# Loading x first, and computing some adaLN rows on TensorE, in the opening of a hybrid decoder block

## The chip, the cores and the metric

The kernel runs on one core of a Trainium2 chip. Its time is the device time of one execution in microseconds. Three runs of the kernel before took 1878.87 to 1883.16 us, median 1879.36.

The engines named here: TensorE (PE; its weight loads are PEld) multiplies matrices; VectorE (DVE) and ScalarE (ACT) work elementwise; GpSimd (POOL) does a few small operations; SyncE (SP) issues DMAs. Each runs its own queue in order and waits on the others through semaphores.

## The reference

One decoder block on x (1024 tokens, 1024 features, float32). Only its first lines matter for this change:

```
mod = silu(c) @ w_ada + b_ada                  # 6 x 1024 values for the sequence
sh1, sc1, g1, sh2, sc2, g2 = split(mod, 6)
h = rms_norm(x, pre_norm1_w) * (1 + sc1) + sh1
proj = h @ w_in                                # z, xbc, dt, q, k, v, gates
```

Then follow a Mamba-2 branch and a differential-attention branch on the parts of proj, their merge by sigmoid gates, an output projection, and a gated convolutional feed-forward network, each with a norm around it. In the attention branch a constant, lambda, is the difference of the exponentials of two dot products of 64 elements.

## The kernel before

All large products are float32 split in two: a high part rounded to a type that TensorE takes at full pace (float32r), and a low part, the difference. A product of two such operands is three TensorE products (high x high, low x high, high x low).

The opening (lines 151 to 324) makes h, transposed (features on partitions), in 16 **units**: 8 feature blocks k of 128, times 2 token halves of 512. It also multiplies each unit by the first three weight blocks (two of w_xbc, one of w_gate), so that TensorE has work while h is made. By steps:

- `load_x`, `square_x`, `rstd_x`, `scale_x`: eight tiles of x (128 tokens x 1024), each 512 KB, are loaded; ScalarE sums their squares; VectorE and GpSimd make the reciprocal root; ScalarE or VectorE scales each tile. A half is four tiles.
- `load_mod(j)`: the two 128-column strips of w_ada that give shift and scale of feature block j, 1 MB, by four DMAs of 256 KB in runs of 512 bytes, into eight buffers (four blocks).
- `mod_sum(j, k)`: VectorE multiplies the k-th 128 rows of these strips by silu(c) and adds them up: eight operations on 128 x 256, and one more that joins two partial sums. `mod_cols(j)`: two TensorE products with a column of ones sum over the partitions and leave shift and scale as columns. `mod_end(j)`: three tiny VectorE operations add the bias and apply the norm weight. Block 0 has a form of its own, `mod_first`: shift by TensorE, with the strips as stationary operand, scale by VectorE.
- `make_h(k, half)`: four TensorE transposes; ScalarE applies scale and shift into float32 (line 240) and rounds a copy of that to the high part (line 241); VectorE subtracts for the low part (line 242).
- `products(k, half)`: nine TensorE products (lines 256 to 258), accumulated over the units in PSUM.

The order within the opening is written out by hand for TensorE, VectorE, ScalarE and SP (`tc.manual_schedule`). Loads: half one of x, block 0 of w_ada, the three weight blocks, block 1, half two of x, blocks 2 and 3, then one w_ada block each time a block has been summed. Units: (0,0), (1,0), (0,1), (1,1), then by block. In unit n TensorE transposes unit n and then runs the products of unit n-1, while VectorE does four sums. A scheduler merges this list with the code that follows it, so that some later instructions stand among those of the opening on VectorE, ScalarE and SP: constants for lambda (lines 1256 to 1260, written after the chunk stage, in no list of their own), a copy of `sel` (line 341), the split of the second w_gate block (lines 93 and 94) and some differences of h (line 557). SP waits, for each DMA, for the one eight before it.

After the opening TensorE goes on to the other w_gate blocks (lines 115 to 117), then to the projections by a Strassen-like scheme, the chunk stage of the Mamba branch, attention, and the feed-forward network.

## Time and profile before

| what | value |
|---|---|
| median of 3 runs | 1879.36 us (1878.87 to 1883.16) |
| profiled execution: time | 1882.31 us |
| profiled execution: span | 1880.2 us |
| TensorE busy | 1837.8 us, 98% |
| VectorE busy | 1301.7 us, 69% |
| ScalarE busy | 889.7 us, 47% |
| mean granted TensorE clock | 0.999 |

A row of the timeline gives start and duration in us, the engine, the source line, the operation, what it writes and reads, the shape, the count of merged instructions, and in brackets how long the engine was idle before it and what ended that. A TensorE product's duration holds the way through the array, so that products overlap: their pace is read from one start to the next. Rows of the windows give, for each stretch, its length and the busy time and instruction count of each engine, the granted clock, the busy share of the DMA engines and what they moved. A row of a group gives smallest, median and largest duration.

### The profile page before, as it was taken

How to read it: one execution, taken by the hardware profiler on the slowest of the kernel's cores; microseconds unless marked ns; L12 is line 12 of the kernel's file. 1: busy time of each engine (PE TensorE's matmuls, PEld its weight loads, DVE VectorE, ACT ScalarE, POOL GpSimd, SP SyncE). 2: the span in 40 equal slices, each digit the busy share in tenths (PEclk: the TensorE clock that was granted, in tenths of full speed). 3: DMA queues.
4: the chain of work that ended last, by engine and by line, in shares of the span. 5: the costliest groups of instructions: out<-in, count | busy, mean ns of one | idle time of the engine just before them, and what ended most of it. 6: DMA issues, size and time to landing. Idle time of an engine off the chain costs nothing.

```text
span 1880.2 us, 24563 instructions
## 1 busy us (share of the span) xinstructions
PE 1837.8 (98%) x9032; PEld 1535.6 (82%) x9032; DVE 1301.7 (69%) x1987; ACT 889.7 (47%) x1718; POOL 145.2 (8%) x137
## 2 busy tenths in 40 slices
PE   6999999999999999999999999999999999999998
PEld 4788889987888888888888888888888888887886
DVE  6777877689755247777667465478898888876545
ACT  5644543345443025656556323465554545455532
POOL 0000000145521000000000000000000000000001
PEclk9999999999999999999999999999999999999999
DMA  9356356678837746666543755122232323278844
GB/s 307 129 180 211 101 177 206 208 275 284 292 118 179 232 140 174 172 192 167 146 135 109 244 190 219 45 90 101 97 120 103 113 90 107 106 233 294 255 150 160
DMA packets 145623, 322.05 MB, mean 171 GB/s; under 512 B 17376, under 2 KB 56928, under 8 KB 145504
## 3 DMA queue, kind: packets, MB, share of 16 engines
q1 hardware_dynamic: 144192, 317.30, 52.1%
q0 software_dynamic: 1312, 3.19, 0.5%
q8 instruction: 71, 1.16, 0.3%
q14 instruction: 48, 0.39, 0.1%
HBM read 225.26 MB, written 95.17 MB: 170 GB/s over the span
## 4 chain that ended last, share of the span: by engine, by line
PE 75%; DVE 12%; DMA 5%; ACT 5%; issue 2%; SPq 1%; POOL 0%; POOLq 0%; ACTq 0%; DVEq 0%
PE upx L1748 3%; PE upx L1747 3%; PE upx L1749 3%; PE o L1438 3%; PE xx L458 2%; PE ao L115 2%; PE so L116 2%; PE xx L459 2%; PE ao L117 2%; PE so L117 2%; PE dx L2111 2%; PE xx L460 2%; PE so L115 2%; PE ao L116 2%; PE dx L2112 2%
## 5 line engine op out<-in xcount | busy, mean ns | idle before, releaser
L1747 PE MATMUL upx<-t,wu_t 128*128 128x512 f32 x264 | 103.3, 391 | 1.1 <-DVE cv L2175 1.0
L1748 PE MATMUL upx<-t,wu_t 128*128 128x512 f32 x264 | 102.9, 390 | 0.2 <-DVE t L1865 0.2
L1749 PE MATMUL upx<-t,wu_t 128*128 128x512 f32 x264 | 102.8, 389 | 0.0
L1721 ACT ACTIVATE wu_t<-sab 128x512 fp32r<-128x512 f32 x57 | 34.1, 627 | 130.1 <-DVE sab L1738 130.1
L1426 ACT COPY aT<-at 128x512 f32<-128x512 f32 (+2 forms) x96 | 46.0, 480 | 102.3 <-PE at L1425 102.3
L94 DVE TENSOR_TENSOR g_lo<-gst,g_hi 128x1024 fp32r<-128x1024 f32 (+1 forms) x42 | 47.5, 1135 | 52.6 <-ACT g_hi L93 52.6
L1438 PEld LDWEIGHTS o<-vt,aT 128*128 128x128 f32 x576 | 74.7, 191 | 9.7 <-ACT aT L1426 5.6
L1438 PE MATMUL o<-vt,aT 128*128 128x128 f32 x576 | 81.0, 277 | 0.3
L93 ACT ACTIVATE g_hi<-gst 128x1024 fp32r<-128x1024 f32 (+1 forms) x42 | 41.5, 988 | 66.8 <-DMA gst<-gld_s 36.9
L1399 DVE TENSOR_REDUCE nmx<-sc 128x1 f32<-128x640 f32 (+3 forms) x64 | 65.6, 1024 | 2.2
L1379 PE MATMUL sc<-kst,qst 128*128 128x512 f32 (+2 forms) x192 | 63.9, 341 | 0.0
L1380 PE MATMUL sc<-klo,qst 128*128 128x512 f32 (+2 forms) x192 | 63.2, 346 | 0.0
L1765 DVE SCALAR_TENSOR_TENSOR ug<-cg,vec,ug 128x1023 f32<-128x1023 f32 (+1 forms) x44 | 56.3, 1280 | 6.8 <-ACT ug L1764 6.0
L1747 PEld LDWEIGHTS upx<-t,wu_t 128*128 128x128 f32 x264 | 49.6, 188 | 12.7 <-DVE cv L2175 2.4
L1748 PEld LDWEIGHTS upx<-t,wu_t 128*128 128x128 f32 x264 | 49.6, 188 | 10.6 <-DVE t L1865 0.5
L1749 PEld LDWEIGHTS upx<-t,wu_t 128*128 128x128 f32 x264 | 49.6, 188 | 10.3
L1725 DVE TENSOR_TENSOR wu_t<-sab,wu_t 128x512 fp32r<-128x512 f32 x57 | 39.3, 690 | 26.5 <-ACT wu_t L1721 26.5
L1765 DVE SCALAR_TENSOR_TENSOR uv<-cv,vec,uv 128x1023 f32<-128x1023 f32 (+1 forms) x44 | 56.2, 1278 | 0.9 <-ACT uv L1764 0.9
L1415 DVE RECIPROCAL rsm<-ssum 128x2 f32<-128x2 f32 x64 | 10.6, 166 | 63.4 <-ACT p L1412 36.0
L142 POOL TENSOR_TENSOR rsf<-rsf,nhalf 128x1 f32<-128x1 f32 x8 | 5.6, 703 | 626.9 <-DVE rsf L141 624.2
L1417 DVE SCALAR_TENSOR_TENSOR p<-p,coef,p 128x128 f32<-128x128 f32 (+3 forms) x64 | 52.4, 819 | 2.3
L1425 PE MATMUL at<-ident,p 128*128 128x128 f32 x288 | 47.8, 275 | 5.9 <-DVE p L1417 5.9
(543 smaller groups left out, 5957.1 us busy)
## 6 DMA issues: line engine op xcount, KB each, us to landing
adas<-in_w_ada SPq DMA_DIRECT2D x32, 512.0 KB, 5.1
wdr<-in_w_down SPq DMA_DIRECT2D x22, 512.0 KB, 5.6
wtd<-wds SPq DMA_DIRECT2D x22, 512.0 KB, 4.3
wuf<-in_w_up SPq DMA_DIRECT2D x22, 512.0 KB, 3.5
gld_s<-gsum SPq DMA_DIRECT2D x22, 512.0 KB, 2.8
gst<-gld_s SPq DMA_DIRECT2D x20, 512.0 KB, 4.7
wdt_raw<-wtd SPq DMA_DIRECT2D x20, 512.0 KB, 4.7
wuv<-in_w_up SPq DMA_DIRECT2D x19, 512.0 KB, 3.5
```

Of the source, the lines that this page charges most:

```text
L115: T.matmul(ps, lh, rh, start=(i == 0), stop=False)
L116: T.matmul(ps, lh, rl, start=False, stop=False)
L117: T.matmul(ps, ll, rh, start=False, stop=(i == n - 1))
L1379: T.matmul(sc[:, n0:n1], qs_[s][:, tsl], ks_[s][:, n0:n1], start=True, stop=False)
L1380: T.matmul(sc[:, n0:n1], qs_[s][:, tsl], kl[s][:, n0:n1], start=False, stop=True)
L1399: V.reduce_max(nmx[:, bq, s : s + 1], sc[:, :L], axis=AX.X, negate=True)
L1417: V.scalar_tensor_tensor(pr[0][:, :L], pr[1][:, :L], coef[:, bq : bq + 1], pr[0][:, :L], op0=ALU.mult, op1=ALU.add)
L1438: T.matmul(po_of[j, grp][:, qi, :], at[:, k, :], vt[j % 2][:, kt, :], start=(kt == 0), stop=(kt == i))
L1747: T.matmul(out_, wh, xh_, start=(k == 0 and first), stop=False, skip_group_check=not first)
L1748: T.matmul(out_, wh, xl_, start=False, stop=False, skip_group_check=not first)
L1749: T.matmul(out_, wl, xh_, start=False, stop=(k == end), skip_group_check=not first)
L1765: V.scalar_tensor_tensor(u[:, d:], c_[:, : S - d], fw[:, 2 - d : 3 - d], u[:, d:], op0=ALU.mult, op1=ALU.add)
```

## The change

- **Loads in another order and layout.** The host stores the shift and scale strips of w_ada as an array of its own, `w_ada1`, in which half of a block is 128 runs of 4 KB; `load_mod` issues two DMAs of 512 KB instead of four of 256. There are six buffers instead of eight (three blocks). The order is now: half one of x, block 0, the first quarter of the three weight blocks, half two of x, block 1, the second quarter, block 2; later block 3 and the last half of the weight blocks.
- **Rows on TensorE.** For blocks 0, 1, 4 and 6, `mod_row` replaces the sums: eight float32 products of a 128 x 1 column of silu(c) with 128 x 256 of the strips give a row in PSUM, VectorE copies it, and two products with a one turn it into columns. Blocks 2, 3, 5 and 7 are summed on VectorE as before. `mod_first` is gone.
- **Constant products.** TensorE multiplies ones by ones (128 columns, float32) 36 times at the start and 16 times behind the first unit; the result is overwritten.
- **Units by block**: (0,0), (0,1), (1,0), and so on. VectorE does four sums in each of the first three units of the loop and two in the later ones.
- **High part straight from PSUM.** ScalarE writes the high part first, then the float32 value, both from PSUM.
- **Weight splits in three parts**, in the first, third and sixth unit and after; the root of the squares by pairs of tiles.
- **Moved constants.** The copy of `sel` goes into the list of the gate stage, the lambda constants into the list of the chunk stage.

In the merged order SP issues the load of the second w_gate block ahead of block 7 of w_ada; its splits stand on ScalarE and VectorE between unit (3,0) and unit (3,1).

```diff
+WARM = 36
+ROWS = (4, 6)
...
+    NADA = 6
...
     def load_mod(j):
         for b in range(2):
-            for g in range(2):
-                SP.dma_start(
-                    adat[(2 * j + b) % 8][:, :, g, :],
-                    a["w_ada"][b * HALF : (b + 1) * HALF, g * D + j * P : g * D + (j + 1) * P].rearrange("(k p) c -> p k c", p=P),
-                )
+            SP.dma_start(adat[(2 * j + b) % NADA].rearrange("p k g c -> p (k g c)"), a["w_ada1"][2 * j + b])
...
+    def mod_row(j):
+        pr = next_bank(f"mrow{j}")
+        row = acc0[j % 2][0:1, 0]
+        for k in range(KD):
+            T.matmul(pr[0:1, : 2 * P], scl[:, k : k + 1], wada(j, k).rearrange("p g c -> p (g c)"), start=(k == 0), stop=(k == KD - 1))
+        V.tensor_copy(row.rearrange("p g c -> p (g c)"), pr[0:1, : 2 * P])
+        mps[j] = next_bank(f"mod{j}")
+        for g in range(2):
+            T.matmul(mps[j][:, 2 * g : 2 * g + 2], row[:, g, :], ones[0:1, 0:2], start=True, stop=True)
...
-        A.activation(xh, ps, AF.Identity, scale=a1[:, k : k + 1], bias=sh1[:, k : k + 1])
-        A.activation(hi, xh, AF.Copy)
+        A.activation(hi, ps, AF.Identity, scale=a1[:, k : k + 1], bias=sh1[:, k : k + 1])
+        A.activation(xh, ps, AF.Identity, scale=a1[:, k : k + 1], bias=sh1[:, k : k + 1])
...
+    def idle(n):
+        for _ in range(n):
+            T.matmul(pg0[1][:, :P], ones, ones, start=True, stop=True)
...
+        for i in range(4):
+            load_x(i)
         load_mod(0)
+        load_first(0, 2)
+        for i in range(4, 8):
+            load_x(i)
         load_mod(1)
+        load_first(2, 4)
         load_mod(2)
+        idle(WARM)
...
+        mod_row(0)
         load_mod(3)
+        load_first(4, 8)
...
+        products(0, 0)
+        idle(16)
...
+        mod_row(1)
...
+        units = [(k, h) for k in range(1, KD) for h in range(2)]
+        last, before = (0, 1), None
         for n, u in enumerate(units):
+            pt0 = turn_x(*u)
+            low = make_h(*u, pt0)
+            done, n_sum = None, 4 if n < 3 else 2
...
+            if n in (0, 3):
+                for b in range(3):
+                    first_high(b, *((2, 4) if n == 0 else (4, 8)))
+            if n == 0:
+                for b in range(3):
+                    first_low(b, 2, 4)
+            elif 3 < n < 7:
+                first_low(n - 4, 4, 8)
+            products(*last)
+            last = u
+            if u[1] == 0 and u[0] + 1 in ROWS:
+                done = u[0] + 1
+                mod_row(done)
+            elif done is not None:
+                mod_cols(done)
+            if done is not None and done + 3 < KD:
+                load_mod(done + 3)
```

More of the change, by code (lines that the diff above doesn't have):

```diff
@@ L154 @@
     junk = SL.get("junk0")
-    adat = [SL.get(f"adat{i}", F32, (P, 4, 2, P)) for i in range(8)]
+    NADA = 6
+    adat = [SL.get(f"adat{i}", F32, (P, 4, 2, P)) for i in range(NADA)]
     acc0 = [SL.get(f"acc0_{i}", F32, (P, 2, 2, P)) for i in range(2)]
@@ L161, with load_x, rstd_x @@
     a1 = const("a1", [P, KD])
-    def load_x(half):
-        for q in range(4):
-            i = 4 * half + q
-            SP.dma_start(xts[i], a["x"][i * P : (i + 1) * P, :])
+    def load_x(i):
+        SP.dma_start(xts[i], a["x"][i * P : (i + 1) * P, :])
     def square_x(i):
         A.activation(junk, xts[i], AF.Square, accum_out=ss1[:, i : i + 1])
-    def rstd_x(half):
-        hs = slice(4 * half, 4 * half + 4)
-        rstd_of(rs1[:, hs], ss1[:, hs], 1.0 / D, 1e-6)
+    def rstd_x(i):
+        rstd_of(rs1[:, i : i + 2], ss1[:, i : i + 2], 1.0 / D, 1e-6)
     def scale_x(i, on_act):
@@ L179, in scale_x, with wada, next_bank @@
             V.tensor_scalar(xts[i], xts[i], rs1[:, i : i + 1], None, op0=ALU.mult)
+    def wada(j, k):
+        return adat[(2 * j + k // 4) % NADA][:, k % 4]
     def load_mod(j):
         for b in range(2):
-            for g in range(2):
-                SP.dma_start(
-                    adat[(2 * j + b) % 8][:, :, g, :],
-                    a["w_ada"][b * HALF : (b + 1) * HALF, g * D + j * P : g * D + (j + 1) * P].rearrange("(k p) c -> p k c", p=P),
-                )
-    mps = {}
-    def wada(j, k):
-        return adat[(2 * j + k // 4) % 8][:, k % 4]
+            SP.dma_start(adat[(2 * j + b) % NADA].rearrange("p k g c -> p (k g c)"), a["w_ada1"][2 * j + b])
+    mps = {}
+    n_b = 0
+    def next_bank(name):
+        nonlocal n_b
+        n_b += 1
+        return (ps_wb, ps_wc)[n_b % 2](name)
+    def mod_row(j):
[7 more added lines that the diff above has]
+            T.matmul(mps[j][:, 2 * g : 2 * g + 2], row[:, g, :], ones[0:1, 0:2], start=True, stop=True)
     def mod_sum(j, k):
@@ L204, in mod_cols @@
     def mod_cols(j):
-        mps[j] = ps_wb(f"mod{j}")
+        mps[j] = next_bank(f"mod{j}")
         for g in range(2):
             T.matmul(mps[j][:, 2 * g : 2 * g + 2], acc0[j % 2][:, 0, g, :], ones[:, 0:2], start=True, stop=True)
-    def mod_first():
-        mps[0] = ps_wb("mod0")
-        acc = acc0[0][:, :, 1, :]
-        for k in range(KD):
-            T.matmul(mps[0][:, 0:2], wada(0, k)[:, 0, :], scl2[:, k, :], start=(k == 0), stop=(k == KD - 1))
-        for k in range(KD):
-            w_ = wada(0, k)[:, 1, :]
-            if k < 2:
-                V.tensor_scalar(acc[:, k % 2], w_, scl[:, k : k + 1], None, op0=ALU.mult)
-            else:
-                V.scalar_tensor_tensor(acc[:, k % 2], w_, scl[:, k : k + 1], acc[:, k % 2], op0=ALU.mult, op1=ALU.add)
-        for h in range(2):
-            T.matmul(mps[0][:, 2:4], acc[:, h], ones[:, 0:2], start=(h == 0), stop=(h == 1))
     def mod_end(j):
@@ L228, in mod_end, with turn_x, make_h @@
         V.scalar_tensor_tensor(a1[:, j : j + 1], a1[:, j : j + 1], 1.0, vec[:, V_PN1 + j : V_PN1 + j + 1], op0=ALU.add, op1=ALU.mult)
-    n_h = 0
-    def make_h(k, half):
-        nonlocal n_h
-        ps = (ps_wb, ps_wc)[n_h % 2](f"xtr{k}_{half}")
+    def turn_x(k, half):
+        ps = next_bank(f"xtr{k}_{half}")
         for q in range(4):
             T.transpose(ps[:, q * P : (q + 1) * P], xts[4 * half + q][:, k * P : (k + 1) * P], ident)
+        return ps
+    def make_h(k, half, ps):
         xh = hr[k // KH][half][k % KH // 2][:, k % 2, :]
-        n_h += 1
         hi, lo = hT[k][half][:, 0, :], hT[k][half][:, 1, :]
+        A.activation(hi, ps, AF.Identity, scale=a1[:, k : k + 1], bias=sh1[:, k : k + 1])
         A.activation(xh, ps, AF.Identity, scale=a1[:, k : k + 1], bias=sh1[:, k : k + 1])
-        A.activation(hi, xh, AF.Copy)
         return lambda: V.tensor_tensor(lo, xh, hi.bitcast(F32), op=ALU.subtract)
@@ L249, with load_first, first_high, first_low @@
     pg0 = [ps_wa("gs0_0"), ps_wa("gs0_1")]
+    def load_first(k0, k1):
+        for b, (n, i) in enumerate(firsts):
+            SP.dma_start(raw0[b][:, k0:k1, :].rearrange("p k c -> p (k c)"), a[n][i][:, k0 * P : k1 * P])
+    def first_high(b, k0, k1):
+        A.activation(w0[b][0][:, k0:k1], raw0[b][:, k0:k1], AF.Copy)
+    def first_low(b, k0, k1):
+        V.tensor_tensor(w0[b][1][:, k0:k1], raw0[b][:, k0:k1], w0[b][0][:, k0:k1].bitcast(F32), op=ALU.subtract)
     def products(k, half):
@@ L258, in products @@
             T.matmul(o, wh, xl_, start=False, stop=(k == KD - 1))
+    def idle(n):
+        for _ in range(n):
+            T.matmul(pg0[1][:, :P], ones, ones, start=True, stop=True)
     EN = mybir.EngineType
     with tc.manual_schedule(engines={EN.PE, EN.DVE, EN.Activation, EN.SP}):
-        load_x(0)
+        for i in range(4):
+            load_x(i)
         load_mod(0)
-        for b, (n, i) in enumerate(firsts):
-            SP.dma_start(raw0[b].rearrange("p k c -> p (k c)"), a[n][i])
+        load_first(0, 2)
+        for i in range(4, 8):
+            load_x(i)
@@ L266 @@
         load_mod(1)
-        load_x(1)
+        load_first(2, 4)
         load_mod(2)
-        load_mod(3)
-        for i in range(4):
-            square_x(i)
-        rstd_x(0)
-        mod_first()
-        for i in range(4):
-            scale_x(i, i < 3)
+        idle(WARM)
+        square_x(0)
+        square_x(1)
+        rstd_x(0)
+        square_x(2)
+        square_x(3)
+        rstd_x(2)
+        scale_x(0, False)
+        scale_x(1, False)
+        mod_row(0)
+        load_mod(3)
+        load_first(4, 8)
@@ L276 @@
+        scale_x(2, True)
+        scale_x(3, False)
+        pt0 = turn_x(0, 0)
         mod_end(0)
-        low = make_h(0, 0)
-        V.tensor_copy(w0[0][0], raw0[0])
-        V.tensor_tensor(w0[0][1], raw0[0], w0[0][0].bitcast(F32), op=ALU.subtract)
+        for b in range(3):
+            first_high(b, 0, 2)
+        low = make_h(0, 0, pt0)
+        first_low(0, 0, 2)
         low()
-        for b in (1, 2):
-            split(w0[b][0], w0[b][1], raw0[b])
+        first_low(1, 0, 2)
+        first_low(2, 0, 2)
@@ L283 @@
+        products(0, 0)
+        idle(16)
         for i in range(4, 8):
             square_x(i)
-        for k in range(KD):
-            mod_sum(1, k)
+            if i % 2:
+                rstd_x(i - 1)
+        for i in (4, 5):
+            scale_x(i, False)
+        mod_row(1)
+        scale_x(6, True)
+        scale_x(7, False)
         load_mod(4)
-        products(0, 0)
-        mod_cols(1)
+        pt0 = turn_x(0, 1)
         mod_end(1)
-        rstd_x(1)
-        sums = [(j, k) for j in range(2, KD) for k in range(KD)]
@@ L293 @@
-        units = [(1, 0), (0, 1), (1, 1)] + [(k, h) for k in range(2, KD) for h in range(2)]
-        last, done_before = (0, 0), None
-        for n, u in enumerate(units):
-            if n == 1:
-                for i in (4, 6):
-                    scale_x(i, True)
-            low = make_h(*u)
-            if n == 0:
-                for i in (5, 7):
-                    scale_x(i, False)
-            done, ready = None, done_before
-            for m in range(4):
-                if m == 2 and ready is not None:
-                    mod_end(ready)
-                if not sums:
-                    continue
-                j, k = sums.pop(0)
-                mod_sum(j, k)
-                if k == KD - 1:
-                    done = j
-                    if j + 3 < KD:
-                        load_mod(j + 3)
-            low()
-            if n > 0:
-                products(*last)
+        low = make_h(0, 1, pt0)
@@ new lines @@
+        low()
+        sums = [(j, k) for j in range(2, KD) for k in range(KD) if j not in ROWS]
+        for _ in range(4):
+            mod_sum(*sums.pop(0))
+        units = [(k, h) for k in range(1, KD) for h in range(2)]
+        last, before = (0, 1), None
+        for n, u in enumerate(units):
+            pt0 = turn_x(*u)
+            low = make_h(*u, pt0)
+            done, n_sum = None, 4 if n < 3 else 2
+            for m in range(n_sum):
+                if 2 * m == n_sum and before is not None:
+                    mod_end(before)
+                if sums:
+                    j, k = sums.pop(0)
+                    mod_sum(j, k)
+                    if k == KD - 1:
+                        done = j
+            low()
+            if n in (0, 3):
+                for b in range(3):
+                    first_high(b, *((2, 4) if n == 0 else (4, 8)))
+            if n == 0:
+                for b in range(3):
+                    first_low(b, 2, 4)
+            elif 3 < n < 7:
+                first_low(n - 4, 4, 8)
+            products(*last)
@@ L318 @@
             last = u
-            if done is not None:
+            if u[1] == 0 and u[0] + 1 in ROWS:
+                done = u[0] + 1
+                mod_row(done)
+            elif done is not None:
                 mod_cols(done)
-            done_before = done
+            if done is not None and done + 3 < KD:
+                load_mod(done + 3)
+            before = done
+        assert not sums
         products(*last)
@@ L340 @@
     sel = const("sel_r", [P, NH], F32R)
-    V.tensor_copy(sel, selr)
     zd = [dp.tile([P, D], F32, tag=f"zd{i}", name=f"zd{i}") for i in range(8)]
@@ L470, in ada_load @@
             ada_of[n_ald] = adas[n_ald % len(adas)]
-            SP.dma_start(ada_of[n_ald], a["w_ada"][k * P : (k + 1) * P, (r + 2) * D : (r + 3) * D])
+            SP.dma_start(ada_of[n_ald], a["w_ada"][k * P : (k + 1) * P, r * D : (r + 1) * D])
             n_ald += 1
@@ L529 @@
     with tc.manual_schedule(engines={EN.PE, EN.DVE, EN.Activation, EN.SP}):
+        V.tensor_copy(sel, selr)
         vev = SL.get("vev", F32, (P, 2, HALF))
@@ L1115 @@
         chunk_mask(0, 1)
+        lamt = const("lamt", [P, 2, 64])
+        lams = const("lams", [P, 2])
+        nlam = const("nlam", [P, 1])
+        rl = rows[:, R_LAM : R_LAM + 256].rearrange("p (a b d) -> p a b d", a=2, b=2)
+        V.tensor_tensor(lamt, rl[:, :, 0, :], rl[:, :, 1, :], op=ALU.mult)
+        V.reduce_sum(lams, lamt, axis=AX.X)
+        A.activation(lams, lams, AF.Exp)
+        V.tensor_tensor(nlam, lams[:, 1:2], lams[:, 0:1], op=ALU.subtract)
+        V.tensor_scalar(nlam, nlam, -LAM_INIT, None, op0=ALU.add)
+        subw = const("subw", [P, 1])
+        V.tensor_scalar(subw, vec[:, V_SUB : V_SUB + 1], 1.0 - LAM_INIT, None, op0=ALU.mult)
         fill(4)
@@ L1249 @@
         SL.put(*yT[k])
-    lamt = const("lamt", [P, 2, 64])
-    lams = const("lams", [P, 2])
-    nlam = const("nlam", [P, 1])
-    rl = rows[:, R_LAM : R_LAM + 256].rearrange("p (a b d) -> p a b d", a=2, b=2)
-    V.tensor_tensor(lamt, rl[:, :, 0, :], rl[:, :, 1, :], op=ALU.mult)
-    V.reduce_sum(lams, lamt, axis=AX.X)
-    A.activation(lams, lams, AF.Exp)
-    V.tensor_tensor(nlam, lams[:, 1:2], lams[:, 0:1], op=ALU.subtract)
-    V.tensor_scalar(nlam, nlam, -LAM_INIT, None, op0=ALU.add)
-    subw = const("subw", [P, 1])
-    V.tensor_scalar(subw, vec[:, V_SUB : V_SUB + 1], 1.0 - LAM_INIT, None, op0=ALU.mult)
     vt = [SL.get(f"vt{i}", F32, (P, 8, P)) for i in range(2)]
@@ L2294, in host_arrays @@
         "cT": np.ascontiguousarray(np.ascontiguousarray(i["c"])[0].reshape(8, 128).T),
-        "w_ada": f("w_ada"),
+        "w_ada": np.ascontiguousarray(f("w_ada")[:, 2048:]),
+        "w_ada1": np.ascontiguousarray(
+            f("w_ada")[:, :2048].reshape(2, 4, 128, 2, 8, 128).transpose(4, 0, 2, 1, 3, 5)
+        ).reshape(16, 128, 1024),
         "b_ada": b_ada[None],
```

## The prediction

> **What bounds the kernel now.** I read the page's first two parts, then busy time by window, then the timeline of TensorE where its idle time lies.

> ```profile
> span 1880.2 us, 24563 instructions
> PE 1837.8 (98%) x9032; PEld 1535.6 (82%) x9032; DVE 1301.7 (69%) x1987; ACT 889.7 (47%) x1718; POOL 145.2 (8%) x137
> ...
> core 0: us, PE busy (x) PEld busy (x) DVE busy (x) ACT busy (x) POOL busy (x), PEclk, DMA share, GB/s
> 0.00:17.20 17.20, 5.59 (x24) 5.18 (x24) 4.69 (x19) 9.31 (x13) 1.22 (x5) 1.00 0.89 300
> 17.20:31.50 14.30, 7.63 (x22) 4.77 (x22) 10.42 (x23) 11.39 (x16) 1.02 (x1) 1.00 1.12 333
> 31.50:35.70 4.20, 4.20 (x16) 3.25 (x14) 3.90 (x10) 1.41 (x2) 0.00 (x0) 1.00 1.17 291
> 35.70:75.80 40.10, 37.93 (x201) 30.51 (x201) 30.18 (x84) 21.26 (x30) 0.00 (x0) 1.00 0.62 185
> 75.80:107.00 31.20, 31.20 (x139) 25.87 (x138) 23.89 (x37) 17.58 (x31) 0.00 (x0) 1.00 0.29 104
> ```

> TensorE is busy 98% of the span. From 75.8 us it has no gap (31.20 of 31.20), so the opening is worth exactly what it moves the start of that stretch, 75.76 below. Before it TensorE loses 11.6 us up to 17.2 and 6.7 us up to 31.5, with the DMA engines full, and only 2.2 us from 35.7 on.

> ```profile
> 18.82 0.80 PE L256 MATMUL xbc<-hT,wf_hi 128*128 128x512 f32 x1 [1.53 <-ACT hT L241]
> ...
> 31.51 0.78 PE L256 MATMUL xbc<-hT,wf_hi 128*128 128x512 f32 x1
> 32.08 0.63 PE L257 MATMUL xbc<-hT,wf_lo 128*128 128x512 f32 x1
> 32.51 0.63 PE L258 MATMUL xbc<-hT,wf_hi 128*128 128x512 f32 x1
> ...
> 36.39 0.40 PE L257 MATMUL xbc<-hT,wf_lo 128*128 128x512 f32 x1
> 36.62 0.39 PE L258 MATMUL xbc<-hT,wf_hi 128*128 128x512 f32 x1
> ...
> 38.22 0.60 PE L236 MATMUL xtr<-ident,xt 128*128 128x128 f32 x4
> 38.57 0.48 PE L256 MATMUL xbc<-hT,wf_hi 128*128 128x512 f32 x1
> ...
> 75.76 0.39 PE L115 MATMUL gs<-hT,wgs_hi 128*128 128x512 f32 x1
> ```

> The opening is 16 units (8 feature blocks, 2 token halves) of 4 transposes and 9 products. The first unit starts at 18.82, the second only at 31.51. Products follow each other at 0.43 us there (32.08 to 32.51) and at 0.23 from 36 on: TensorE is slow until about 35.5, though the granted clock reads 1.00 in all windows. A fast unit is 9 x 0.23 + 0.44 = 2.5 us.

> The 44.25 us from 31.51 to 75.76 hold 15 units less one set of transposes, 15 x 2.5 - 0.35 = 37.15; six pairs of column products (blocks 2 to 7), 6 x 0.44 = 2.6, from 59.70 to 60.14 below; the slow pace, 9 x 0.20 = 1.8; and so about 2.7 of waits, of which these rows show the largest two:

> ```profile
> 49.84 0.29 DVE L1256 TENSOR_TENSOR lamt<-rows 128x128 f32<-128x128 f32 x1 [1.57 <-DMA rows<-in_rows]
> ...
> 51.11 0.50 PE L258 MATMUL xbc<-hT,wf_hi 128*128 128x512 f32 x1 [0.86 <-DVE hT L242]
> ...
> 59.14 0.42 DVE L202 TENSOR_TENSOR acc<-acc 128x256 f32<-128x256 f32 x1
> ...
> 59.70 0.58 PE L207 MATMUL mod<-ones,acc 128*128 128x2 f32 x4 [0.75 <-DVE acc L202]
> 60.14 0.52 PE L236 MATMUL xtr<-ident,xt 128*128 128x128 f32 x3
> ```

> **The change, part by part.**

> *Price of a row product.* A row is 8 float32 products of 256 columns. The nearest rows are the float32 products of line 811, one product of 512 columns recorded as two passes (two products are x4):

> ```profile
> 273.23 1.88 PE L811 MATMUL adar<-accr,ones 128*128 128x512 f32 x4
> 274.54 0.72 PE L115 MATMUL z<-wz_hi,hT 128*128 128x346 f32 x1
> 275.10 0.32 PE L116 MATMUL z<-wz_lo,hT 128*128 128x346 f32 x1
> 275.26 0.32 PE L117 MATMUL z<-wz_hi,hT 128*128 128x346 f32 x1
> ```

> From 273.23 to 275.10 lie four passes and one L115 (0.16, as 275.10 to 275.26): 1.71 us, 0.43 a pass of 512 columns. A pass of 256 is 0.215, a product 0.43, a row 8 x 0.43 = 3.44 us. Lower bound: one pass of a 512-column float32r product takes 0.23, so 256 columns 0.115 and a row 0.9. I take 3.44, since the operation and the type are the same. Behind a row TensorE waits for VectorE's copy: tail 0.16 (0.39 less 0.23), copy 0.42 (as L202), handover 0.14 (from 59.14 + 0.42 to 59.70), 0.72 in all; then the two column products, 0.44. The copy also waits for what VectorE has queued before it, which for blocks 4 and 6 ends while the row runs.

> *Loads and the first unit.*

> ```profile
> 5.88 1.06 ACT L169 ACTIVATE junk<-xt 128x1024 f32<-128x1024 f32 x1 [3.30 <-DMA xt<-in_x]
> ...
> 10.24 1.06 ACT L169 ACTIVATE junk<-xt 128x1024 f32<-128x1024 f32 x1 [0.20 <-DMA xt<-in_x]
> ...
> 22.50 1.06 ACT L169 ACTIVATE junk<-xt 128x1024 f32<-128x1024 f32 x1 [1.84 <-DMA xt<-in_x]
> ...
> 26.44 1.06 ACT L169 ACTIVATE junk<-xt 128x1024 f32<-128x1024 f32 x1 [0.17 <-DMA xt<-in_x]
> ...
> DMA to landing us min/median/max: 3.7/6.4/7.8
> ```

> Tiles of x, 512 KB in 4 KB runs, land 1.31 us apart ((26.44 - 22.50) / 3), 400 GB/s; the w_ada pieces alone run at 291 (the window 31.5 to 35.7), and the new array moves them in runs of 4 KB too. From 5.88 on at 1.31, the two halves of block 0 land at 11.1 and 12.4, and the second half of x, behind 0.4 MB of first weights, at about 15 to 19 instead of 22.5 to 26.4. SP issues half as many w_ada DMAs; each still waits for the one eight before it, which costs nothing while the engines are full. A constant product (128 columns, two passes) is half a row product, 0.215 fast and 0.43 slow. The 36 of them start at about 1 us, the first 4 us slow (9 of them), the others 27 x 0.215: done at 10.8, before the row. Sum: 11.1 + 3.44 + 0.72 + 0.44 + transposes 0.44 + the first ACT pass 0.78 = 17.0 for the first product, 1.8 earlier.

> [...]

> *Wait for the second half.* Unit one ends at 17.0 + 1.0 (its low part, below) + 2.07 = 20.1. Sixteen constant products, 16 x 0.215 = 3.4, hold TensorE to 23.5; the squares of the second half (4 x 1.28 from about 18) end beside them. Row 1: 23.5 + 3.44 + 0.72 + 0.44 + 0.44 + 0.78 = 29.3 for the first product of the second unit, against 31.51, and at full pace (1.8 more). Lead: 4.0 us.

> *The rest.* From 29.3: 15 units 37.15; column products for blocks 2, 3, 5 and 7, 4 x 0.44 = 1.8; rows 4 and 6, 2 x (3.44 + 0.72 + 0.44) = 9.2. With no wait at all that ends at 77.45, already later than 75.76.

> New waits come from these durations:

> ```profile
> 44.35 0.78 ACT L240 ACTIVATE hr<-xtr,sh,a 128x512 f32<-128x512 f32 x1 [1.08 <-PE xtr L236]
> ...
> 45.95 0.68 DVE L242 TENSOR_TENSOR hT<-hr,hT 128x512 fp32r<-128x512 f32 x1
> ...
> 43.91 1.67 DVE L200 SCALAR_TENSOR_TENSOR acc<-adat,scl,acc 128x256 f32<-128x256 f32 x4
> ...
> 41.09 0.61 DVE L198 TENSOR_SCALAR acc<-adat,scl 128x256 f32<-128x256 f32 x2
> ...
> 51.93 1.04 ACT L93 ACTIVATE wgs_hi<-wgs_raw 128x1024 fp32r<-128x1024 f32 x1
> ...
> 54.36 1.21 DVE L94 TENSOR_TENSOR wgs_lo<-wgs_raw,wgs_hi 128x1024 fp32r<-128x1024 f32 x1
> ...
> DMA to landing us min/median/max: 4.3/5.1/6.7
> ```

> The high part now comes from the first ACT pass (0.6 us earlier than by a copy), the low part 0.78 + 0.68 later; where a unit has no other work ahead, its third product waits 1.0. That holds for unit two: 1.0. Block 2's eight sums start behind that low part: 0.6 + 6 x 0.4 + 0.4 = 3.4 us, while TensorE needs 2.07 for the unit: 1.7 of wait at its column products, 0.3 more for block 3. The load of the second gate block needs a buffer that is free only after VectorE's last-quarter split of the first weight block (about 47 us); it lands 3.7 us later (the fastest x tile; the last row above, that of the w_gate loads, gives 4.3 to 6.7). ScalarE's and VectorE's splits of it, 1.04 + 1.21, stand ahead of unit (3,1)'s passes on both queues, so that unit's third product comes 1.2 late, and products of three units and column products 5 are queued behind it. Sum 4.2, between 1.0 (all but the first hidden) and 7.2 (6.7 in place of 3.7).

> *Moved constants.* Four VectorE operations (0.9 us) and one ScalarE exponential go from the opening to the chunk stage, where VectorE has gaps and TensorE none:

> ```profile
> 366.00:382.00 16.00, 15.98 (x92) 13.14 (x91) 13.62 (x18) 11.78 (x34) 7.09 (x7) 1.00 0.50 166
> ```

> Zero, at most 0.9 if that cover goes. The wait for the rows at 49.84 is gone, in the old 2.7.

> Sum: 29.3 + 37.15 + 1.8 + 9.2 + 4.2 = 81.65, against 75.76: **5.9 us later**. The profiled execution took 1882.31 us (span 1880.2), so 1888.2 against its own; it is 2.95 above the median of the runs, 1879.36, which gives **1885.3**.

> A point on the pace: here slow products end some 4 us after TensorE became busy without gaps (31.51 to about 35.5). [...]

> **Rivals.** (1) *The waits are hidden and the lead is kept*: VectorE's queue drains faster than I order it, so 2 to 4 us of the 4.2 go; 1881.3 to 1883.3. For it: VectorE is idle a quarter of 35.7 to 75.8. Against: the first two waits stand right behind late data. (2) *The gate load, or a slow start, costs more*: 6.7 instead of 3.7 us of landing adds 3.0, constant products that stay slow for 7 us, as the whole first unit did at 18.82, another 1.0; 1886.3 to 1889.3. For it: w_gate's median of 5.1, and that nothing before 11 us shows the pace. (3) *Faster: a row with a one-column stationary runs at the bound of 0.115 a product.* Rows 1, 4 and 6 would each fall by 2.5, together 7.6: 1877.7. It decides from a product below 0.18 us (5.9 / 24 less than 0.43). For it: no row shows a one-column stationary. Against: line 811 gives 0.43 for 256 columns. (4) *The order of loads does nothing*: unit two starts at 31.5 though warm, because splits and not x gate it; then 2.2 us worse, 1887.5; against it, the 13.9 us between unit starts hold 3.9 us of product only.

> **How the numbers follow.** From no change a measurement can tell about 0.3%, 5.6 us here (1873.7 to 1885.0). My case has 0.50, its own range 1883 to 1888, a third of all chance above 1885.0 and 0.17 below; rival 1 has 0.18; rivals 2 and 4 0.22; rival 3 0.10, of which 0.06 for a gain over 5.6: with rival 1 beside it the gain is 4.7 to 5.7. Slower 0.33 + 0.22 = 0.55, same 0.17 + 0.18 + 0.04 = 0.39, faster 0.06. Range 1878.5 to 1890.

> **What would show it.** First product near 17.0 and second unit near 29.3; products 0.23 apart from the start; four rows of 16 passes, each row 3.4 us; idle time of TensorE on VectorE at rows and at block 2; ScalarE waiting for the w_gate load at about 48 to 51; first line-115 product (its new number) near 81.7. I am wrong if rows take under 2 us, if TensorE slows again in the wait for x, or if the stretch behind the opening is no longer without gaps.

## The result, and the profile after

The changed kernel took 1889.9 us (median of 1888.76 to 1894.34); runs of the kernel before beside it took 1880.78. The ratio is 1.0054, 95% interval 1.0038 to 1.0069: slower, by 9.1 us between the medians, where 5.9 was forecast. The profiled execution took 1891.74 us, with a span of 1890.0. One execution of a run below, the profiled one of e6, had a granted clock of 0.654 over its whole span and took 2639.40 us, where the other nine took 1877.82 to 1884.87: it is left out of e6's median, and no time is read from its trace.

First the page of the changed kernel: its span, and busy time of each engine.

```profile
span 1890.0 us, 24839 instructions
...
PE 1861.6 (98%) x9184; PEld 1551.3 (82%) x9184; DVE 1294.0 (68%) x1966; ACT 885.6 (47%) x1720; POOL 147.4 (8%) x139
```

TensorE has 24 us more work and the span grew by 9.8. Next its timeline of TensorE in the opening (start, duration, engine, line, operation, output and inputs, shape, count, and the idle time before). The line numbers are those of the new file: 201 the rows, 205 their columns, 220 the column products of a block summed on VectorE, 231 the transposes, 263 to 265 the nine products, 270 the constant products, 117 the first line of what follows the opening (115 before).

```profile
1.06 10.17 PE L270 MATMUL gs<-ones 128*128 128x128 f32 x72 [1.06 <-DVE nhalf L140]
11.90 3.61 PE L201 MATMUL mrow<-adat,scl 128*1 128x256 f32 x16 [0.68 <-DMA adat<-in_w_ada]
16.02 0.60 PE L205 MATMUL mod<-ones,acc 1*128 1x2 f32 x4 [0.51 <-DVE acc L202]
16.55 0.66 PE L231 MATMUL xtr<-ident,xt 128*128 128x128 f32 x4
18.08 0.50 PE L263 MATMUL xbc<-hT,wf_hi 128*128 128x512 f32 x1 [0.87 <-ACT hT L237]
18.41 0.41 PE L264 MATMUL xbc<-hT,wf_lo 128*128 128x512 f32 x1
19.47 0.79 PE L265 MATMUL xbc<-hT,wf_hi 128*128 128x512 f32 x1 [0.65 <-DVE hT L239]
20.07 0.63 PE L263 MATMUL xbc<-hT,wf_hi 128*128 128x512 f32 x1
20.49 0.63 PE L264 MATMUL xbc<-hT,wf_lo 128*128 128x512 f32 x1
...
22.63 5.09 PE L270 MATMUL gs<-ones 128*128 128x128 f32 x32
27.65 3.61 PE L201 MATMUL mrow<-adat,scl 128*1 128x256 f32 x16
31.86 0.57 PE L205 MATMUL mod<-ones,acc 1*128 1x2 f32 x4 [0.60 <-DVE acc L202]
32.37 1.10 PE L231 MATMUL xtr<-ident,xt 128*128 128x128 f32 x8
33.89 0.50 PE L263 MATMUL xbc<-hT,wf_hi 128*128 128x512 f32 x1 [0.42 <-ACT hT L237]
...
35.29 0.50 PE L265 MATMUL xbc<-hT,wf_hi 128*128 128x512 f32 x1 [0.66 <-DVE hT L239]
...
38.74 0.62 PE L220 MATMUL mod<-ones,acc 128*128 128x2 f32 x4 [1.56 <-DVE acc L215]
...
87.17 0.39 PE L117 MATMUL gs<-hT,wgs_hi 128*128 128x512 f32 x1
```

The opening ends at 87.17 us, 11.4 later than the 75.76 of before. Its first unit starts 0.7 earlier than before, its second 2.4 later. The waits in the brackets aren't all of it; the pace shows the rest. From 20.07 to 20.49 two products are 0.42 apart, where the fast pace is 0.23. The 16 constant products (32 passes) take 5.09 us, 0.159 a pass; in the run e11 below, with the clock full from 6.76 us on, the same 32 take 3.73. (The 72 passes at the start took 10.17 us, and there the clock records show full clock only from 5.01 us on, so that the first four of those ten were slow: 0.213 us a pass up to 4.85 us, 0.112 from 5.04 on.) The windows of the same kernel say what happened (length, busy time and count of each engine, granted clock, DMA share, GB/s):

```profile
core 0: us, PE busy (x) PEld busy (x) DVE busy (x) ACT busy (x) POOL busy (x), PEclk, DMA share, GB/s
12.00:16.00 4.00, 3.52 (x16) 1.17 (x14) 1.70 (x4) 2.07 (x4) 1.29 (x1) 1.00 0.97 356
16.00:20.00 4.00, 2.46 (x11) 1.73 (x12) 2.63 (x8) 2.72 (x5) 0.00 (x0) 0.83 1.03 413
20.00:24.00 4.00, 4.00 (x14) 3.35 (x13) 0.96 (x4) 3.21 (x6) 1.15 (x2) 0.50 1.04 392
24.00:28.00 4.00, 4.00 (x29) 3.70 (x29) 0.81 (x2) 1.15 (x1) 0.84 (x1) 0.81 1.03 404
...
36.00:40.00 4.00, 2.44 (x15) 1.90 (x13) 3.97 (x11) 0.76 (x3) 0.00 (x0) 0.89 0.49 146
40.00:44.00 4.00, 4.00 (x17) 3.24 (x16) 3.97 (x13) 1.48 (x3) 0.00 (x0) 0.68 0.56 198
44.00:48.00 4.00, 4.00 (x23) 3.45 (x22) 2.14 (x8) 2.54 (x4) 0.00 (x0) 1.00 0.79 243
```

Of the 11.4 us of the opening 9.5 are left at the end. The same product, counted from the last one, is 10.7 us late at 343 us (time of before), 9.8 at 652, 10.8 at 1718 and 9.5 from 1765 on. The last step of 1.3 is also there (1.4) in the run e8 below, which has nothing of the change but constant products: it belongs to the profiled execution of before.

### The profile page after: what moved, and what is told of

Same layout as the page of the kernel before. It is cut to its first block, busy times and chain, and to the rows that moved or that the text cites. A ratio compares the mean times of both kernels' runs of the same rounds, so it can differ in the third digit from the quotient of the medians.

```text
span 1890.0 us, 24839 instructions
## 1 busy us (share of the span) xinstructions
PE 1861.6 (98%) x9184; PEld 1551.3 (82%) x9184; DVE 1294.0 (68%) x1966; ACT 885.6 (47%) x1720; POOL 147.4 (8%) x139
## 4 chain that ended last, share of the span: by engine, by line
PE 77%; DVE 11%; ACT 5%; DMA 5%; issue 2%; SPq 0%; POOL 0%; POOLq 0%; DVEq 0%; ACTq 0%
PE upx L1784 3%; PE upx L1785 3%; PE upx L1783 3%; PE o L1474 3%; PE dx L2147 2%; PE dx L2148 2%; PE dy L2147 2%; PE dy L2148 2%; PE dx L2146 2%; PE dy L2146 2%; PE ao L117 2%; PE so L118 2%; PE ao L119 2%; PE so L117 2%; PE so L119 2%
```

## The experiments

All times are medians, with the ratio to the kernel before in the same set of runs and its 95% interval. "Opening ends" is the start of the first product of line 117 (115 in the order of before) in the run's profiled execution.

| run | what | opening ends | us | ratio |
|---|---|---|---|---|
| before | | 75.76 | 1879.4 to 1881.0 | 1 |
| changed | | 87.17 | 1889.9 | 1.0054 (1.0038 to 1.0069) |
| e1 | rows with a full stationary | 85.35 | 1890.72 | 1.0056 (1.0041 to 1.0071) |
| e2 | waits around row 0 filled | 84.68 | 1888.68 | 1.0047 (1.0032 to 1.0062) |
| e11 | block 2's wait filled too | 83.36 | 1887.40 | 1.0039 (1.0025 to 1.0052) |
| e4 | no constant products | 83.45 | 1888.26 | 1.0045 (1.0030 to 1.0059) |
| e3 | no rows 4 and 6 | 78.95 | 1882.82 | 1.0015 (1.0005 to 1.0025) |
| e5 | e3, waits around row 0 filled | 78.06 | 1880.74 | 1.0000 (0.9991 to 1.0010) |
| e10 | e5, block 2's wait filled too | 77.08 | 1882.00 | 1.0006 (0.9997 to 1.0015) |
| e6 | e5 without the 16 constant products | - | 1879.18 | 0.9995 (0.9985 to 1.0005) |
| e7 | e6, four sums ahead of row 1 | 73.93 | 1880.15 | 0.9995 (0.9985 to 1.0004) |
| e9 | e6, four sums still earlier | 75.50 | 1881.03 | 1.0001 (0.9992 to 1.0010) |
| e12 | e6, four sums ahead of the low part | 72.14 | 1879.23 | 0.9992 (0.9983 to 1.0001) |
| e8 | the kernel before, with constant products | 76.01 | 1881.46 | 1.0005 (0.9996 to 1.0014) |

**What makes the clock fall?** Theory A: the rows. A product with one stationary column (128*1 in the rows, where others have 128*128) might not count as work. Theory B: the waits around the row, 0.68, 0.51, 0.87 and 0.65 us within 8 us. e1 gives the rows a full stationary (the same column 128 times, the row then stands on every partition), e2 leaves the rows and fills two waits.

```diff
-            T.matmul(pr[0:1, : 2 * P], scl[:, k : k + 1], wada(j, k)...
+            T.matmul(pr[:, : 2 * P], scl[:, k : k + 1].broadcast_to([P, P]), wada(j, k)...
```

> Edit: the row products take the column of silu(c) repeated 128 times as their stationary operand, so all 128 columns of the array work instead of one; columns streamed, copies and waits stay. Theory A (one-column products do not count as work for the clock, so it falls to half after a row): the slow stretches at 18.7 to 25.5 us and 39.1 to 42.6 us go, unit one takes 3.1 us instead of 4.6, the 16 constant products 3.4 instead of 5.0, the second unit starts near 30.8 instead of 33.9, the opening ends at 82.8 to 84.2 instead of 87.2, the time falls by 3 to 4.4 us to about 1886. Theory B (the gaps of TensorE at the copy and before the first product let the clock fall): nothing changes, opening 87, time 1890.

```diff
         V.tensor_copy(row.rearrange("p g c -> p (g c)"), pr[0:1, : 2 * P])
+        if j == 0:
+            idle(3)
...
+        idle(4)
         products(0, 0)
```

> Edit: the rows stay one column wide; three constant products fill TensorE's gap at the copy of row 0, four more the gap before the first product. Theory A (one-column products cool the clock): the slow stretch after row 0 stays, the opening ends at 87 to 88. Theory B (the gaps do): the stretch at 18.7 to 25.5 is gone, unit one takes 3.1 us, the second unit starts near 31, the opening ends near 84.5 and the time is about 1887.

The windows of e1, then those of e2, and of e1's timeline the first row:

```profile
16.00:20.00 4.00, 2.37 (x13) 1.28 (x11) 2.14 (x7) 2.06 (x4) 0.00 (x0) 1.00 1.02 415
20.00:24.00 4.00, 3.59 (x11) 2.94 (x12) 1.20 (x4) 3.91 (x7) 0.70 (x1) 0.57 1.05 392
...
12.76 3.69 PE L201 MATMUL mrow<-adat,scl 128*128 128x256 f32 x16 [0.73 <-DMA adat<-in_w_ada]
```

```profile
16.00:20.00 4.00, 3.34 (x25) 2.60 (x23) 2.34 (x8) 2.27 (x3) 0.00 (x0) 1.00 1.03 412
20.00:24.00 4.00, 4.00 (x29) 3.73 (x29) 0.95 (x5) 3.67 (x8) 0.70 (x1) 1.00 1.04 393
...
36.00:40.00 4.00, 3.59 (x16) 2.99 (x17) 3.96 (x13) 1.45 (x2) 0.00 (x0) 0.71 0.58 202
40.00:44.00 4.00, 4.00 (x22) 3.31 (x21) 2.82 (x7) 1.45 (x2) 0.00 (x0) 0.86 0.72 209
```

With a full stationary the clock still falls behind row 0 (0.57 in the window from 20), and a row costs the same, 3.69 against 3.61, so one column isn't to be had at a lower price. e1 by itself doesn't settle A: its fall lasts 3.41 us instead of 6.83, it has none at block 2, and its opening ends at 85.35, between what A gave (82.8 to 84.2) and what B gave (87). With seven constant products in two waits the first fall is gone, the second unit starts at 31.56 instead of 33.89, and the opening ends 2.5 us earlier. The second fall, behind the wait for block 2's sums, stays. The time, 1888.68 us, is above the 1887 that was expected. Here the first fall disappears although the rows are one column wide, and that puts A out. So does e4 below: there the clock rises at 17.77 us, behind 3.41 us in which TensorE did nothing but passes of a one-column row.

**What are the constant products worth?** e4 takes them all out.

```diff
-        idle(WARM)
...
-        idle(16)
```

> Edit: no constant products at all (neither the 36 nor the 16). If they keep TensorE fast: row 0 runs at half pace (6.9 us instead of 3.4), first product near 21.5 instead of 18.1, row 1 again slow, the second unit near 35 to 36 and slow for some 4 us, opening 89 to 91, time 1892 to 1894. Rival (they serve nothing, and the 16 are 5 us in the way of row 1): opening near 83, time 1886.

The opening ends at 83.45 us, as the rival has it, and the time is 1888.26 us, above the rival's 1886 and no slower than with the constant products. Its TensorE at the first row, and at row 1:

```profile
11.78 6.56 PE L201 MATMUL mrow<-adat,scl 128*1 128x256 f32 x16 [11.78 <-DMA adat<-in_w_ada]
...
25.16 3.61 PE L201 MATMUL mrow<-adat,scl 128*1 128x256 f32 x16
```

The 36 at the start do make row 0 fast (3.61 against 6.56). But row 1 starts at 25.16 without a wait, 2.5 us earlier than in the changed kernel: its data was there, and the 16 constant products kept it waiting.

**What do rows 4 and 6 cost?** e3 sums blocks 4 and 6 on VectorE again, four sums in each unit; rows 0 and 1 stay.

```diff
-ROWS = (4, 6)
+ROWS = ()
...
-            done, n_sum = None, 4 if n < 3 else 2
+            done, n_sum = None, 4
```

> Edit: blocks 4 and 6 are summed on VectorE (four sums in every unit), so only rows 0 and 1 stay on TensorE. By the prediction's price a row costs 3.44 + 0.72 and its column products as before, so two rows are 8.3 us of TensorE's path; VectorE's waits come back with 1 to 3 us: opening ends at 80 to 82 instead of 87.2, time 1883 to 1885. Rival (the rows replace waits of VectorE of the same size, and the loss is all in the clock and the start): opening 86 to 87, time 1889.

The opening ends at 78.95 and the run takes 1882.82 us, a little below the 80 to 82 and 1883 to 1885 expected: about 7 of the 9 us are gone. Not all of that is the rows. In the opening the clock of this trace is at half for 3.41 us, that of the changed kernel for 10.24; e10 and e11 below give the price of the rows without any fall.

**Is it the share of time in which TensorE works?** In these traces the clock records change only at multiples of 3.41 us from the first one (the changed kernel's at 5.01, 18.66, 25.49, 39.14 and 42.55 us). In every trace of this case but e6's I cut the span into stretches on that grid, and for each one at full clock took the share in which a product ran and the clock of the next (stretches that begin after 1860 us left out):

| share of a stretch at full clock | next one full | next one half |
|---|---|---|
| under 0.575 | 0 | 8 |
| 0.575 to 0.62 | 11 | 3 |
| over 0.62 | 7017 | 0 |

In the changed kernel the stretches ahead of the falls have 0.60 and 0.54; the first lies in the band in which the share alone doesn't decide. The longest single wait of a stretch sorts them less well: one with a wait of 1.41 us kept the clock (e4, from 34.84, share 0.587), and the one ahead of the first fall had none above 0.87. The rule by share was found from the runs (theory C), so the next runs put it to a test. e5 is e2 and e3 together; e10 and e11 fill the wait for block 2's sums as well, without and with rows 4 and 6.

> Rows 4 and 6 go back to sums on VectorE, and the two waits around row 0's handover are filled with constant products (3 and 4). Theory C, the clock falls to half behind a stretch of some 3.4 us in which TensorE worked about 60% or less: no fall near 20 us, first product near 18.6, second unit near 31.5 (as with the fill alone), and from there 45.6 us as in the run with sums alone: the line-117 products start near 77.2, 78.6 if a later wait lets the clock fall once; 1880.5 to 1882 us. Theory D, the fall near 20 us does not come from the waits: it is there again, second unit near 33.3, opening ends near 79, 1882.8 us as with the sums alone.

```diff
     def mod_cols(j):
         mps[j] = next_bank(f"mod{j}")
+        if j == 2:
+            for _ in range(8):
+                T.matmul(mps[j][:, :P], ones, ones, start=True, stop=True)
```

> As e5, with 8 constant products in the wait for block 2's sums. Theory C (the clock falls behind a 3.4 us stretch in which TensorE worked about 60% or less): no fall at 37 us, the products behind that wait take 2.3 us and not 3.7, the line-117 products start near 76.6 instead of 78.1, and TensorE's clock is full from 6 us to the end; 1879.4 us. Theory D (a fall comes anyway some 30 us after the start): half clock again for 3.4 us before 45 us, 78 and 1880.7 us.

> The changed kernel with all its parts, rows 4 and 6 too, and constant products in the three waits behind which the clock fell (3, 4 and 8). Theory C: no fall; first product near 18.5, second unit near 31.5, line-117 products near 83.2 instead of 87.2 and 84.7 (with the first two waits filled), 1887 to 1888 us. What then still lies above the forecast's 81.65 is the late first row and the length of the 16 constant products, and not the clock. Theory D: as with two waits filled, 84.7, 1888.7 us.

The constant products at the start of e11, its row 0, its windows, and where its opening ends:

```profile
1.06 11.01 PE L275 MATMUL gs<-ones 128*128 128x128 f32 x72 [1.06 <-DVE nhalf L140]
12.00 3.62 PE L201 MATMUL mrow<-adat,scl 128*1 128x256 f32 x16
...
20.00:24.00 4.00, 4.00 (x29) 3.71 (x30) 0.95 (x5) 3.57 (x8) 0.75 (x2) 1.00 1.05 393
...
32.00:36.00 4.00, 3.34 (x21) 2.85 (x21) 3.84 (x10) 2.35 (x6) 0.00 (x0) 1.00 0.28 88
36.00:40.00 4.00, 4.00 (x28) 3.47 (x26) 3.97 (x14) 1.52 (x3) 0.00 (x0) 1.00 0.61 209
...
83.36 0.39 PE L117 MATMUL gs<-hT,wgs_hi 128*128 128x512 f32 x1
```

e11 and e10 have no fall before the last 5 us of their spans; e5 has the one at 37 us that was allowed for. The ends of the openings are within 0.9 us of what theory C gave (77.2 to 78.6, 76.6 and 83.2 expected; 78.06, 77.08 and 83.36 found). D is out. The times are less sharp: e11 at 1887.40 is in the expected 1887 to 1888, but e10, for which 1879.4 was expected and whose opening is 1.0 us shorter than e5's, took 1882.00, 1.3 more than e5. The intervals of the two overlap, so that single microsecond isn't seen in the times.

**The kernel before with constant products alone.** e8 adds 36 at the start, and 6, 8 and 10 ahead of the first unit's products, block 1's columns and the second unit's transposes.

```diff
+        idle(36)
         load_x(0)
...
+        idle(6)
         products(0, 0)
+        idle(8)
         mod_cols(1)
...
             if n == 1:
+                idle(10)
```

> The kernel before, with constant products only: 36 at its start, 6 ahead of the first unit's products, 8 ahead of block 1's column products and 10 ahead of the second unit's transposes. Nothing else moves. If a warm clock by itself is worth what the second unit lost to half pace (3.97 against 2.3 us): line-115 products at 74.0 instead of 75.8, 1877.5 us. If the waits at 50 to 66 us (0.9, 0.3, 0.8, 0.3), which do not depend on TensorE's pace, take the lead back: 75.3 to 75.8, 1879 us, no change.

Neither branch: the second unit is slow all the same. Its timeline there:

```profile
25.94 2.40 PE L262 MATMUL gs<-ones 128*128 128x128 f32 x20
31.04 0.69 PE L236 MATMUL xtr<-ident,xt 128*128 128x128 f32 x2 [2.71 <-ACT xt L177]
32.08 0.69 PE L236 MATMUL xtr<-ident,xt 128*128 128x128 f32 x2 [0.35 <-ACT xt L177]
32.42 0.78 PE L256 MATMUL xbc<-hT,wf_hi 128*128 128x512 f32 x1
32.99 0.63 PE L257 MATMUL xbc<-hT,wf_lo 128*128 128x512 f32 x1
```

At full pace ten constant products are over in 2.4 us, and 2.71 us of waiting for ScalarE's scaling of x remain: the clock falls at 30.88 (and once before, at 17.23). These were as good as none, and 1881.46 us against 1880.59 is no change.

**What is left of the change without its dear parts.** e6, e7, e9 and e12 have no rows 4 and 6, filled waits around row 0, and no 16 constant products; they differ in where VectorE makes block 2's first four sums, and e9 and e12 also have three constant products behind row 1.

```diff
-        idle(16)
...
         low = make_h(0, 1, pt0)
-        low()
         sums = [(j, k) for j in range(2, KD) for k in range(KD) if j not in ROWS]
         for _ in range(4):
             mod_sum(*sums.pop(0))
+        low()
```

(This is e12; e6 has the sums behind `low()`, e7 ahead of `mod_row(1)`, e9 behind the first pair of the second half's squares, and three more constant products ahead of the second unit's products.)

> As e5, and without the 16 constant products ahead of row 1. If they, and not the data, hold row 1 back: row 1 starts at about 22 us instead of 25.3, the second unit near 28.6, and the line-117 products near 74.2 to 75.8, about the 75.8 of the kernel before; 1878 to 1880 us. If VectorE's sums, which start only behind the second unit's low part, set the pace behind it, or if row 1 waits for its half of w_ada instead: opening end near 77, 1881 us as e5.

> As e6, and block 2's first four sums are issued ahead of row 1, where VectorE stood idle for 3.7 us, instead of behind the second unit's low part. If block 2's wait of 1.6 us is VectorE's order of work: it goes, and with it most of the later 0.3 to 0.7 at blocks 4 to 6: the line-117 products start at 72.5 to 74, 1876.5 to 1878.5 us, faster than the kernel before. If the wait comes from the load of block 2's weights, the sums hold VectorE before row 1's copy and the opening is no earlier than in e6: 74 to 76, 1878 to 1880 us.

> As e6 (no rows 4 and 6, waits around row 0 filled, no 16 constant products), with block 2's first four sums put where VectorE waits for ScalarE's last squares, and three constant products each behind row 1's handover and ahead of the second unit's products. If these sums fit into that wait (2.2 us against 1.5) and the clock doesn't fall: row 1 ends at 25.4, its copy is no longer 1.1 late, the second unit starts near 28.5 at full pace, and the line-117 products near 72, against 73.9 in e7 and 75.8 before; 1876 to 1878 us, a ratio of 0.998. If block 2's weights come later than 22 us: VectorE holds the scaling of x up, the copy comes as late as in e7, 73.5 to 75, and 1879 to 1880 us.

> As e6 (no rows 4 and 6, the waits around both handovers filled with three or four constant products, no 16 constant products), with block 2's first four sums between the second unit's scale columns and its low part, where VectorE waits about 2 us for ScalarE, and where block 2's weights (which landed at 25.7 us in e9) are there. If the data's arrival and VectorE's order are all that holds the opening: row 1 at 22.1, its handover without extra delay, the second unit's first product near 28.3 at full pace, little or no wait at block 2, line-117 products near 72 to 72.5 against 75.8 before; 1876.5 to 1878.5 us, a ratio near 0.9985. If the clock still falls once, 1 us later: 73.5 and a ratio of 0.9995, as e6 and e7.

e6's 1879.18 us is in the 1878 to 1880 expected, but where its row 1 and its second unit start isn't known. In e7 block 2's wait goes down to 0.25 us and the opening ends at 73.93, as the first branch has it; the time, 1880.15 us, does not come down to the 1876.5 to 1878.5 of that branch. e7's sums stand ahead of the copy of row 1, which comes 1.1 us late, and the clock falls once. e9 shows what the data allows; VectorE, then TensorE:

```profile
25.71 0.61 DVE L213 TENSOR_SCALAR acc<-adat,scl 128x256 f32<-128x256 f32 x2 [4.39 <-DMA adat<-in_w_ada]
...
28.43 0.40 DVE L202 COPY acc<-mrow 1x256 f32<-1x256 f32 x1
```

```profile
22.14 3.61 PE L201 MATMUL mrow<-adat,scl 128*1 128x256 f32 x16 [0.56 <-DMA adat<-in_w_ada]
...
28.98 0.57 PE L207 MATMUL mod<-ones,acc 1*128 1x2 f32 x4 [2.36 <-DVE acc L202]
```

Block 1 lands at 22.1 us and block 2 at 25.7, and VectorE, in order, held the scaling of x (to 27.10 us) and the copy (to 28.43) behind block 2's sums: the second of the branches written down, with an opening (75.50) and a time (1881.03 us) slightly beyond it. In e12 the sums stand where their data is there:

```profile
21.84 3.61 PE L201 MATMUL mrow<-adat,scl 128*1 128x256 f32 x16
...
28.31 0.50 PE L265 MATMUL xbc<-hT,wf_hi 128*128 128x512 f32 x1 [0.42 <-ACT hT L239]
...
31.84 0.58 PE L222 MATMUL mod<-ones,acc 128*128 128x2 f32 x4 [0.26 <-DVE acc L217]
...
72.14 0.39 PE L117 MATMUL gs<-hT,wgs_hi 128*128 128x512 f32 x1
```

The second unit starts at 28.31 at full pace, block 2 costs 0.26 us, and the opening is 3.6 us shorter than before, as expected. In the time 1.6 of it arrive, less than the 1876.5 to 1878.5 us expected: 1879.23 us against 1880.83, 0.9992 (0.9983 to 1.0001), in the best case a gain of 0.17% and not told from none. Its profiled execution is 2.7 us ahead of that of before at 343 us and 1.6 at the end; what takes the difference behind the opening I didn't settle.

## Why the prediction was right or wrong

The sign was right, and the mechanism of the cost mostly; the size was short by 5.5 us at the end of the opening (81.65 forecast, 87.17 found). Of the 4.6 us between the times themselves (1885.3 and 1889.9) 1.4 are not the change: the kernel before, taken at 1879.36, ran at 1880.78 beside it. Step by step, with e11, the same kernel without the falls of the clock:

| start of | forecast | changed | e11 |
|---|---|---|---|
| row 0 | 11.1 | 11.90 | 12.00 |
| first product | 17.0 | 18.08 | 18.47 |
| 16 constant products | 20.1 | 22.63 | 21.58 |
| row 1 | 23.5 | 27.65 | 25.24 |
| second unit's first product | 29.3 | 33.89 | 31.48 |
| line 117 | 81.65 | 87.17 | 83.36 |

- **The step that failed** is "products 0.23 apart from the start": unit one at 2.07 us, the 16 constant products at 3.4, and the second unit "at full pace" all take it that a TensorE made fast by the constant products stays fast. Two of the waits that the same sum lists around the row, the handover (0.72 forecast, 0.51 found) and ScalarE's pass (0.78 and 0.87), lower its working share to 0.60 of a stretch, and the clock fell; the wait of 1.7 at block 2 (1.56 found) lowers it to 0.54, and it fell again. The wait for the low part comes behind the first fall and lies in a stretch with a share of 0.81, after which the clock stayed at half. Without the falls the end is 3.81 us earlier (87.17 to 83.36): that is 3.8 of the 5.5. The condition "if TensorE slows again in the wait for x" named it among what would make the forecast wrong, but not in the sum, and the second rival had the slow pace only at the start. No run with constant products at its start shows the 7 us of it for which that rival adds 1.0: from the first of them, at 1.06 us, to full clock it lasted 4.0 us in the changed kernel and 5.7 in e11.
- **The rest, 1.7 us**, by e11: row 0 0.9 late; from row 0 to the first product 6.47 us, with seven constant products in it (6.18 in the changed kernel, 5.82 summed); the 16 constant products 3.66 where 3.4 were summed; from row 1 to the second unit 6.24 (5.82 summed). From the second unit on e11 needed 51.88 us against 52.35. In the changed kernel row 0 starts behind its half block, which landed at 11.77 and not at 11.1. In e11 the half block landed at 11.52, and the 36 constant products, slow up to 6.76, held row 0 to 12.00. The sum had them end at 10.8, with the slow pace for the first 4 us.
- **The price of a row** was right: 3.44 forecast, 3.61 with the tail. The third rival (0.115 a product, faster) is out: a row's 16 passes take 3.61 us with one stationary column and 3.69 with 128 (e1). Rows 4 and 6 together cost 6.28 us of the opening (e11 against e10) and 5.4 us of the time; 9.2 less their two column products (0.88) and less the three waits for sums that they spare (0.70, 0.72 and 0.30 in e10) gives 6.6.
- **The new waits**, 4.2 in the sum: the low part 0.66 (1.0 forecast), block 2 1.56 (1.7; as the prediction writes it, 3.4 less 2.07, it would be 1.3), block 3 none (0.3; 0.28 in e11). The second gate block came late as forecast: ScalarE waited 5.02 us for its load, to 56.23. But unit (3,1)'s third product was only 0.3 us late, not 1.2. Row 4, whose 4.7 us ahead of it (51.35 to the transposes at 56.06) held TensorE itself back, may have hidden the rest; this isn't shown, since in e10, without row 4, that product waits 0.30 too, behind a load for which ScalarE waited 0.67.
- **The order of loads** was right in kind: the second half of x comes earlier, at 16.4 to 21.3 us (15 to 19 forecast), and w_ada moves faster (halves of 512 KB land 1.28 us apart from 26.26 on, and the window from 24 to 28 has 404 GB/s, where 291 were measured before). The forecast had the second unit 2.2 us earlier than before and at full pace, 1.8 more; e12, where nothing else stands in the way, starts it 3.2 earlier, at full pace. In the changed kernel the 16 constant products ate it: row 1's data is there at about 22 us (e9; its first half landed at 22.58 in the changed kernel), and they keep TensorE until 27.65. The forecast took them for a filler "beside" the squares and never asked when row 1 could have started. The fourth rival, that the order does nothing, had the result at the second unit (31.48 in e11) for another reason.
- **Moved constants**: no run separates them.
- **"The opening is worth exactly what it moves"** holds only nearly. The changed kernel is 11.40 us late at 107 us (time of before) and 10.72 at 200; e12 is 3.63 ahead at 107, 3.28 at 200 and 2.69 at 343. And one slip in the rivals: the third with the first beside it gains 3.7 to 5.7 us by the prediction's own figures, not 4.7 to 5.7.

So the 11.4 us of the opening are, by the ends of the openings: 3.6 us gained by e12, which keeps the new order and layout of loads, rows 0 and 1, the first 36 constant products, the units by block, the high part from PSUM, the weight splits and the moved constants, not told apart; mainly the 16 constant products and the sums' place, 4.9 lost (e12 to e10); rows 4 and 6 6.3 lost (to e11); the clock 3.8 lost (to the changed kernel).

## What to carry to other kernels

Where the traces show that an engine's clock follows its work, sum the waits of each stretch before using the fast pace in it: here two waits under 1 us, 0.51 and 0.87, in one stretch of 3.41 us stood ahead of a fall to half. A filler on an in-order engine is only free up to the moment when the next real work could start, so look up the landing of that work's data first (the 16 constant products here held row 1 from about 22 to 27.65 us); and one that covers part of a wait may buy nothing, as in e8, where 2.71 us of waiting remained. Work moved from an idle engine to the busiest one cost about its full length here, less the waits that it removed: 6.28 us found for rows 4 and 6, 6.6 reckoned so.

## What the runs showed of the hardware that was not expected

- The clock fell without a long wait. The largest single wait in the stretch ahead of the fall at 18.66 us was 0.87 us, in the one ahead of the fall at 39.14 us 1.56; by share of a 3.41 us stretch at full clock, all 8 under 0.575 were followed by half clock and none of the 7017 over 0.62.
- In these runs it took more work to rise than to stay up. Behind a stretch at half clock with a working share of 0.81 (changed kernel, from 18.66) or 0.85 (e8, from 30.88) the clock stayed at half; it rose behind 0.83 (e3), 0.88 and more. Between 0.81 and 0.88 the share alone doesn't sort these stretches. Passes of a one-column row raised it (e4, at 17.77 us). In the kernel before, a stretch wholly busy with products of two columns (from 11.2 us, on the grid carried back from its first record) didn't: the four transposes behind it, from 16.21, take 1.09 us, against 0.66 at full clock in the changed kernel.
- Where the stretches lie was not the same from one run to the next: in the runs with constant products at the start the first rise came 5.0 to 7.2 us after the start of the span, and the later changes lay on the grid of 3.41 us from it. e1, whose waits on TensorE are nearly those of the changed kernel, had its clock at half for 3.41 us against 10.24, and its opening ends 1.8 us earlier; that the place of the stretches is the reason fits the table above, but no run shows it alone.
- The windows of the kernel before read a clock of 1.00 while its products were 0.43 apart, up to 35 us: its records start at 35.1, with the first rise. The pace of the products is the safer reading.
